# A hybrid decoder layer on one core: a scalar-engine root at the start, evacuations and column sums one by one behind low parts, and another pace in the first feed-forward stage

## The chip, the core and the metric

The kernel runs on one core of one Trainium2 chip. The metric is the device time in microseconds (us). A core has TensorE (PE in the profile, PEld for its weight loads), VectorE (DVE), ScalarE (ACT), GpSimd (POOL) and SyncE (SP, which here only starts DMAs). The engines run their own instruction streams in order and wait for one another by semaphores. PSUM is the memory in which TensorE accumulates; it has eight banks of 128 x 512 floats here.

## The reference, cut to what matters

```python
def swiglu(h, wg, wu, wd):
    return (jax.nn.silu(h @ wg) * (h @ wu)) @ wd

cond = jax.nn.silu(c)
mod = cond @ ada_w[l] + ada_b[l]                 # 9 vectors of 2048
sh1, sc1, gt1, sh2, sc2, gt2, sh3, sc3, gt3 = jnp.split(mod, N_MOD, axis=-1)
h = ada_in(x, norm_g[l, 0], sh1, sc1)            # rmsnorm(x) * (1 + sc1) + sh1
x = x + MACARON_W * gt1[:, None, :] * swiglu(h, ffn_w_gate[l, 0], ffn_w_up[l, 0], ffn_w_down[l, 0])
h = ada_in(x, norm_g[l, 1], sh2, sc2)
x = x + gt2[:, None, :] * hybrid_mixer(h, ...)   # two kinds of attention heads
h = ada_in(x, norm_g[l, 2], sh3, sc3)
x = x + MACARON_W * gt3[:, None, :] * swiglu(h, ffn_w_gate[l, 1], ...)
```

There are 256 tokens, a width of 2048 (16 slices of 128) and a feed-forward width of 5632 (44 slices), all in float32.

## The kernel before, in words

**Weights.** The weights come as 674 blocks of 512 KB, eight tiles of 128 x 128 each, in the order in which TensorE uses them (`Stream.next`, L136). SP starts the DMA of a block into `wraw` (L129), ACT rounds it to the high part `whi` (L133), DVE subtracts to get the low part `wlo` (L147). A product is then high by high, high by low and low by high. Each of the three tiles has four buffers, so the three steps can run some four blocks ahead of TensorE; `wraw` has a fifth. Blocks 0 and 1 are used whole, without parts (L630).

**Columns.** The vectors `mod` are made beside this: one column slice `adat` of 1 MB is fetched (L275) and DVE multiplies it by `cs` and sums it (L279, two rows in the profile, the second reads the sum out). There are 144 of them, 16 for each of nine vectors. `RATE` (L37) says how many columns are begun with each block from a given block on; `ada_need` begins those that are still missing. The columns of scale and shift of slice k make the k-th slice of `h` (`first_h`, L605: ACT, ACT, ACT, then the low part `hs` on DVE); `xrt` (L602) is `x` by its root, two slices at a time.

**Stages.** Blocks 0 to 111 are the gate and up products of the first 28 slices of the first feed-forward net (`gate_up_first`), blocks 112 to 167 its down product, 168 to 231 gate and up of the other 16 slices, 232 to 263 their down product. The mixer follows, then the second feed-forward net. In the first stage the slices of `h` come one by one with the columns, so the products of four groups of slices (8, 8, 8 and 4) are cut into `PIECES` (L24), each a group and the range of k that it adds. At the end of a piece its PSUM banks are emptied: ACT copies them to `acc` (L647) where k starts at 0, DVE adds them (L649, L651) otherwise. After the last piece of a slice come SiLU, the product of gate and up (L548) and the split into `hid` (L534 ACT, L535 DVE). Evacuations that are owed wait in the list `owed`, and `done` (L669) takes from it until at most n are left.

**Order.** The program is written in one order, and a scheduler with a model of its own sorts each engine's instructions by it; `issue_after` binds one instruction behind another. A changed wait can so move instructions far behind the edit.

**Start.** `fv` is the mean square of `x` for the first norm; its inverse root `fy` is made on DVE by `rsqrt` (L304 to L311, eight small instructions), while ACT makes `cs` (L744) and moves the transposed `x` (L769). `fy` becomes a row (`frb`, `nrow`). DVE sums the first two columns in halves (`first_col`, L780) and forms the first slice `h0` (L588, L589), on which TensorE's first product waits.

## Time and profile before

| what | value |
|---|---|
| median of 3 runs | 1918.75 us (1918.09 to 1921.13) |
| the profiled execution, its own time | 1916.67 us |
| its span from the first to the last instruction | 1914.9 us |
| PE busy | 1888.3 us (99%) |
| DVE busy | 1535.9 us (80%) |
| ACT busy | 1030.6 us (54%) |
| mean granted TensorE clock | 0.998 |

Busy TensorE is no TensorE at its peak: a matmul's end is modelled, and the next one starts before it. So the prediction counts the matmuls that begin in a stretch: in stretches of the same kind of product, fewer of them is time lost.

### The profile page before, as it was taken

Reading aid. Unit: us, or ns where it says so; the run is one execution under the profiler, and the core shown is the slowest. Engines: PE = TensorE matmul, PEld = TensorE weight load, DVE = VectorE, ACT = ScalarE, POOL = GpSimd, SP = SyncE. Lnnn points to the kernel's source line nnn. Section 1 sums busy time; section 2 is a strip of 40 time slices with the busy share of each in tenths; the row PEclk is TensorE's granted clock in tenths of the full one; section 3 lists DMA queues with packets and bytes.
Section 4 is the critical chain, followed back from the end, with each engine's and each line's share of the span. In section 5 each row is a group of like instructions: output and inputs, shape, how many; then the busy total and the mean of one; then the engine's idle time right before and its main releaser. Section 6 shows DMA issues by size and latency. Waiting matters only on the chain.

```text
span 1914.9 us, 33495 instructions
## 1 busy us (share of the span) xinstructions
PE 1888.3 (99%) x13090; PEld 1768.2 (92%) x13090; DVE 1535.9 (80%) x2243; ACT 1030.6 (54%) x1623; POOL 56.5 (3%) x50
## 2 busy tenths in 40 slices
PE   8999999999999999999999999999999999999998
PEld 7999999899999989989989999999999999999998
DVE  7999888998999997879978869977777656666654
ACT  8544545433554446756647656655554445555553
POOL 0000000000000120000000002000000000000011
PEclk9999999999999999999999999999999999999999
DMA  9999877999998986687677557777777666666653
GB/s 380 353 358 352 302 268 281 354 403 363 350 341 345 350 324 213 228 302 254 238 258 266 208 186 273 244 259 267 266 259 262 219 200 203 201 200 201 203 201 122
DMA packets 128913, 519.64 MB, mean 271 GB/s; under 512 B 18153, under 2 KB 21481, under 8 KB 110577
## 3 DMA queue, kind: packets, MB, share of 16 engines
q1 hardware_dynamic: 128754, 517.49, 75.2%
q8 instruction: 103, 1.69, 0.4%
q14 instruction: 56, 0.46, 0.1%
HBM read 512.96 MB, written 4.47 MB: 270 GB/s over the span
## 4 chain that ended last, share of the span: by engine, by line
PE 79%; DVE 11%; issue 3%; DMA 3%; ACT 3%; SPq 0%; DVEq 0%; ACTq 0%
PE pd L514 13%; PE pg L510 10%; PE pu L510 10%; PE pd L515 7%; PE pu L511 5%; PE pg L511 5%; DVE wlo L147 4%; PE pgu L635 3%; PE pgu L633 3%; PE pgu L634 3%; DVE adat L279 2%; PE pp L867 2%; PE pp L865 2%; PE pp L866 2%; PE po L514 2%
## 5 line engine op out<-in xcount | busy, mean ns | idle before, releaser
L147 DVE TENSOR_TENSOR wlo<-wraw,whi 128x1024 fp32r<-128x1024 f32 x672 | 819.6, 1226 | 271.8 <-ACT whi L133 270.7
L133 ACT CAST whi<-wraw 128x1024 fp32r<-128x1024 f32 x672 | 698.8, 1046 | 495.7 <-PE pd L514 181.8
L514 PE MATMUL pd<-hid,whi 128*128 128x512 f32 x1370 | 449.6, 382 | 0.8 <-DVE hid L535 0.8
L515 PE MATMUL pd<-hid,wlo 128*128 128x256 f32 x1370 | 374.4, 273 | 2.5 <-DVE wlo L147 2.5
L279 DVE CUSTOM_DVE_ANT_0 adat<-adat,cs,colt 128x2048 f32<-128x2048 f32 x142 | 335.5, 2363 | 11.9 <-DMA adat<-in_ada_dram 11.6
L510 PE MATMUL pg<-hs,whi 128*128 128x512 f32 x912 | 302.0, 382 | 0.5 <-DVE shc L459 0.5
L510 PE MATMUL pu<-hs,whi 128*128 128x512 f32 x912 | 301.8, 382 | 0.0
L514 PEld LDWEIGHTS pd<-hid,whi 128*128 128x128 f32 x1370 | 258.9, 189 | 36.9 <-DVE hid L535 1.1
L515 PEld LDWEIGHTS pd<-hid,wlo 128*128 128x128 f32 x1370 | 263.0, 192 | 5.1 <-DVE wlo L147 4.8
L511 PE MATMUL pu<-hs,wlo 128*128 128x256 f32 x912 | 248.6, 273 | 0.0
L511 PE MATMUL pg<-hs,wlo 128*128 128x256 f32 x912 | 248.6, 273 | 0.0
L633 PE MATMUL pgu<-hs,whi 128*128 128x256 f32 x880 | 241.6, 276 | 2.3 <-ACT whi L133 2.1
L634 PE MATMUL pgu<-hs,whi 128*128 128x256 f32 x880 | 240.9, 275 | 0.0
L635 PE MATMUL pgu<-hs,wlo 128*128 128x256 f32 x880 | 238.6, 276 | 2.2 <-DVE wlo L147 2.2
L510 PEld LDWEIGHTS pg<-hs,whi 128*128 128x128 f32 x912 | 172.4, 189 | 24.9 <-ACT shc L458 0.7
L510 PEld LDWEIGHTS pu<-hs,whi 128*128 128x128 f32 x912 | 172.4, 189 | 24.0
L865 PE MATMUL pp<-hs,whi 128*128 128x256 f32 x656 | 188.2, 288 | 0.0
L867 PE MATMUL pp<-hs,wlo 128*128 128x256 f32 x656 | 181.0, 276 | 1.4 <-DVE wlo L147 1.4
L866 PE MATMUL pp<-hs,whi 128*128 128x256 f32 x656 | 180.9, 276 | 0.0
L511 PEld LDWEIGHTS pu<-hs,wlo 128*128 128x128 f32 x912 | 175.1, 192 | 0.0
L511 PEld LDWEIGHTS pg<-hs,wlo 128*128 128x128 f32 x912 | 175.1, 192 | 0.0
L633 PEld LDWEIGHTS pgu<-hs,whi 128*128 128x128 f32 x880 | 168.9, 192 | 3.0 <-ACT whi L133 2.5
(338 smaller groups left out, 2587.0 us busy)
## 6 DMA issues: line engine op xcount, KB each, us to landing
wraw<-in_w_dram SPq DMA_DIRECT2D x674, 512.0 KB, 4.5
adat<-in_ada_dram SPq DMA_DIRECT2D x142, 1024.0 KB, 7.6
xr<-in_xr_dram SPq DMA_DIRECT2D x4, 512.0 KB, 5.1
adaf<-in_ada_dram SPq DMA_DIRECT2D x4, 512.0 KB, 8.2
xd<-x SPq DMA_DIRECT2D x4, 512.0 KB, 7.6
rw<-rowd SPq DMA_DIRECT2D x16, 128.0 KB, 6.5
x<-xd SPq DMA_DIRECT2D x4, 512.0 KB, 4.9
out_dram<-o SPq DMA_DIRECT2D x4, 512.0 KB, 3.6
```

Source lines behind the costliest of these rows:

```text
L133: self.cast = self.act = self.nc.scalar.copy(h, r).ins
L147: lo_ = nc.vector.tensor_tensor(self.l, r, self.h.bitcast(F32), ALU.subtract)
L279: W.sum = V.tensor_tensor_reduce(t, t, cs, 1.0, L("adab", q, 1), ALU.mult, ALU.add, mod[:, q : q + 1]).ins
L510: PE.matmul(ps, wt[0], both, start=(k == 0), stop=False)
L511: PE.matmul(ps[:, T:], wt[1], part(k, HI), start=False, stop=(k == KD - 1))
L514: PE.matmul(ps, wt[0], act.rearrange("p q (a b) -> p q b a", a=2), start=first, stop=False)
L515: PE.matmul(ps[:, :T], wt[1], woven(act[:, 0]), start=False, stop=last)
L633: PE.matmul(o, wh, part(k, HI), start=first and s == 0, stop=False, skip_group_check=skip)
L634: PE.matmul(o, wh, part(k, LO), start=False, stop=False, skip_group_check=skip)
L635: PE.matmul(o, wl, part(k, HI), start=False, stop=last, skip_group_check=skip)
L865: PE.matmul(pp[i][:, :T], wh, hh, start=(k == 0), stop=False)
L867: PE.matmul(pp[i][:, :T], wl, hh, start=False, stop=(k == KD - 1))
```

## The change

- `PIECES`: the fourth group takes k = 0 and 1 first and k = 2 with its next piece (before: k = 0 to 2, then from 3).
- `RATE`: other numbers up to block 264; the count of columns begun by then is 98 in both.
- Start: `fy` is a square root on ACT with one Newton step on DVE; the first half column stands ahead of that step, and the scaling of `gains_` is bound behind the first split.
- `W.late` is now set with the 33rd column (`i >= 2 * KD`), not with the mixer: from there a sum goes into the list `owing` and is written after a later block's low part. `BEHIND` is 1 until the mixer and 2 from there on (before: 2, in the mixer and behind it alone, since nothing was owed ahead of it). `ada_need` still empties the list wherever it is called.
- `done` takes at most one evacuation at a time where a piece runs slice by slice, and a last evacuation is bound behind the latest low part (`W.split`).

```diff
-    (0, 0, 1, 1), (1, 0, 1, 1), (2, 0, 2, 2), (3, 0, 3, 3), (0, 1, 4, 4), (1, 1, 6, 6), (3, 3, 7, 7),
+    (0, 0, 1, 1), (1, 0, 1, 1), (2, 0, 2, 2), (3, 0, 2, 2), (0, 1, 4, 4), (1, 1, 6, 6), (3, 2, 7, 7),
...
-RATE = ((0, 0.5), (8, 0.4), (50, 0.42), (75, 0.16), (112, 0.42), (168, 0.38), (232, 0.42), (264, 0.0), (284, 0.285), (376, 0.0), (424, 0.16))
+RATE = ((0, 0.44), (24, 0.41), (75, 0.2), (118, 0.42), (232, 0.3), (264, 0.0), (284, 0.285), (376, 0.0), (424, 0.16))
...
-BEHIND = 2
+BEHIND = (1, 2)
...
-                    self.settle(b - BEHIND)
+                    self.settle(b - BEHIND[self.quick])
...
         q = m * KD + j
+        W.late = i >= 2 * KD
...
+        with tc.issue_after(split0):
+            V.tensor_scalar(gains_, gains_, XS, None, ALU.mult)
...
-                V.tensor_add(acc[f], ps, acc[f])
+                with tc.issue_after(W.split):
+                    V.tensor_add(acc[f], ps, acc[f])
                 hids.append(swi(acc[f][:, :T], acc[f][:, T:], hp))
...
-            def done(f, n):
+            def done(f, n, most=NF):
                 owed.append(lambda ps=pb[f], k0=k0, k1=k1: evacuate(ps, f, k0, k1))
-                while len(owed) > n:
+                while len(owed) > n and most:
                     owed.pop(0)()
+                    most -= 1
...
-                    done(f, 1)
+                    done(f, 1, 1)
...
-    V.tensor_scalar(fv, fv, XS * XS / D, XS * XS * EPS, ALU.mult, ALU.add)
-    fy = rsqrt(fv, [P, 2], "x")
+    fy, fh, fa = (ep.tile([P, 2], F32, name=n) for n in ("fy", "fh", "fa"))
+    V.tensor_scalar(fh, fv, -0.5 * XS * XS / D, -0.5 * XS * XS * EPS, ALU.mult, ALU.add)
+    with tc.issue_after(hold):
+        hold = sqrt_table(L("eps")).ins
+    with tc.issue_after(hold):
+        hold = A.activation(fy, fv, AF.Sqrt, bias=L("eps"), scale=XS * XS / D).ins
...
-    first = rs["last"]
+    with tc.issue_after(first):
+        first = first_col(0, 0)
+    with tc.issue_after(first):
+        V.reciprocal(fy, fy)
+    V.tensor_tensor(fa, fy, fy, ALU.mult)
+    V.tensor_tensor(fa, fa, fh, ALU.mult)
+    first = V.scalar_tensor_tensor(fy, fa, 1.5, fy, ALU.add, ALU.mult).ins
...
-    for i, q in ((0, 0), (0, 1), (1, 0), (1, 1)):
+    for i, q in ((0, 1), (1, 0), (1, 1)):
         with tc.issue_after(first):
             first = first_col(i, q)
-    with tc.issue_after(first):
-        V.tensor_scalar(gains_, gains_, XS, None, ALU.mult)
...
-        W.late = True
+        W.quick = 1
```

Three places show what this does to the engines' own orders. First ACT, where TensorE is at blocks 8 to 11 (`acc<-pgu` is an evacuation of a bank, `whi` the rounding of a block, `g1f`, `ht` and `hs` make a slice of `h`). Before:

```order
L609 ACTIVATE g1f<-mod,colt 128x1
L133 CAST whi<-wraw 128x1024 x2
L610 ACTIVATE ht<-xrt,mod,g1f 128x256
L611 CAST hs<-ht 128x2x128
L647 COPY acc<-pgu 128x512 x8
L133 CAST whi<-wraw 128x1024 x3
```

and after:

```order
L612 CAST hs<-ht 128x2x128
L133 CAST whi<-wraw 128x1024
L648 COPY acc<-pgu 128x512 x5
L133 CAST whi<-wraw 128x1024
L648 COPY acc<-pgu 128x512 x3
L133 CAST whi<-wraw 128x1024
```

The eight evacuations of the third group stood in a row behind a slice of `h` and ahead of the casts of blocks 9 to 11; now the casts of blocks 8 and 9 stand between and behind them, and the slice of `h` (k = 2) comes later.

Second DVE from the low part of block 111 on, at the end of the first stage (`acc<-pgu,acc` evacuates, `acc<-acc` is gate by up, `hid` a low part of the result, the two ISA rows one column sum). Before:

```order
L147 TENSOR_TENSOR wlo<-wraw,whi 128x1024
L548 TENSOR_TENSOR acc<-acc 128x256
L279 ISA adat,mod<-adat,cs,colt 128x2048
L279 ISA mod 128x1
L535 TENSOR_TENSOR hid<-acc,hid 128x256
L651 TENSOR_TENSOR acc<-pgu,acc 128x512
L147 TENSOR_TENSOR wlo<-wraw,whi 128x1024
L548 TENSOR_TENSOR acc<-acc 128x256
L147 TENSOR_TENSOR wlo<-wraw,whi 128x1024
L535 TENSOR_TENSOR hid<-acc,hid 128x256
L651 TENSOR_TENSOR acc<-pgu,acc 128x512
L147 TENSOR_TENSOR wlo<-wraw,whi 128x1024
```

and after:

```order
L147 TENSOR_TENSOR wlo<-wraw,whi 128x1024
L547 TENSOR_TENSOR acc<-acc 128x256
L147 TENSOR_TENSOR wlo<-wraw,whi 128x1024
L534 TENSOR_TENSOR hid<-acc,hid 128x256
L653 TENSOR_TENSOR acc<-pgu,acc 128x512
L147 TENSOR_TENSOR wlo<-wraw,whi 128x1024
L547 TENSOR_TENSOR acc<-acc 128x256
L653 TENSOR_TENSOR acc<-pgu,acc 128x512
L534 TENSOR_TENSOR hid<-acc,hid 128x256
L280 ISA adat,mod<-adat,cs,colt 128x2048
L280 ISA mod 128x1
L547 TENSOR_TENSOR acc<-acc 128x256
```

The column sum stood ahead of the low part of block 112 and now stands behind that of block 113. From block 105 to 116 there were four sums (behind blocks 107, 111, 114 and 116), and now there is one (behind 113); another now stands ahead of block 105.

Third DVE from the low part of block 246 on, in the second down product (`x<-pd,mod,x` adds a result to `x`). Before:

```order
L147 TENSOR_TENSOR wlo<-wraw,whi 128x1024
L279 ISA adat,mod<-adat,cs,colt 128x2048
L279 ISA mod 128x1
L540 SCALAR_TENSOR_TENSOR x<-pd,mod,x 128x256
L147 TENSOR_TENSOR wlo<-wraw,whi 128x1024
L542 SCALAR_TENSOR_TENSOR x<-pd,mod,x 128x256
L147 TENSOR_TENSOR wlo<-wraw,whi 128x1024
L279 ISA adat,mod<-adat,cs,colt 128x2048
L279 ISA mod 128x1
L540 SCALAR_TENSOR_TENSOR x<-pd,mod,x 128x256
L147 TENSOR_TENSOR wlo<-wraw,whi 128x1024
L542 SCALAR_TENSOR_TENSOR x<-pd,mod,x 128x256
```

and after:

```order
L147 TENSOR_TENSOR wlo<-wraw,whi 128x1024
L541 SCALAR_TENSOR_TENSOR x<-pd,mod,x 128x256
L280 ISA adat,mod<-adat,cs,colt 128x2048
L280 ISA mod 128x1
L147 TENSOR_TENSOR wlo<-wraw,whi 128x1024 x2
L539 SCALAR_TENSOR_TENSOR x<-pd,mod,x 128x256
L280 ISA adat,mod<-adat,cs,colt 128x2048
L280 ISA mod 128x1
L541 SCALAR_TENSOR_TENSOR x<-pd,mod,x 128x256
L147 TENSOR_TENSOR wlo<-wraw,whi 128x1024 x2
L539 SCALAR_TENSOR_TENSOR x<-pd,mod,x 128x256
L147 TENSOR_TENSOR wlo<-wraw,whi 128x1024
```

Here the sums move behind the low parts by a little. Over the whole stage, from block 232 to 263, there are eleven sums before and nine after.

## Rows read from the trace of the kernel before

**Rows 1.** The page, first part: busy us, share of the span, instructions.
```profile
PE 1888.3 (99%) x13090; PEld 1768.2 (92%) x13090; DVE 1535.9 (80%) x2243; ACT 1030.6 (54%) x1623; POOL 56.5 (3%) x50
```

**Rows 2.** Stretches: their length, busy us of PE, PEld, DVE, ACT, POOL (instructions), clock, DMA.
```profile
26.00:106.00 80.00, 76.70 (x674) 75.66 (x673) 74.49 (x79) 47.10 (x69) 0.00 (x0) 1.00 0.90 354
120.00:200.00 80.00, 80.00 (x719) 80.00 (x718) 74.35 (x77) 38.35 (x49) 0.00 (x0) 1.00 0.96 376
236.00:316.00 80.00, 79.25 (x709) 79.02 (x708) 67.14 (x86) 39.40 (x59) 0.00 (x0) 1.00 0.75 262
350.00:410.00 60.00, 60.00 (x368) 55.24 (x367) 54.47 (x55) 24.16 (x23) 0.00 (x0) 1.00 0.98 383
660.00:720.00 60.00, 57.87 (x346) 51.72 (x345) 58.31 (x63) 27.05 (x36) 15.99 (x11) 1.00 0.90 332
```

**Rows 3.** PE's waits from 26 to 106 us: total us, times, longest.
```profile
PE pgu L633 <- ACT whi L133: 2.1, 2, 1.4
PE pgu L635 <- DVE wlo L147: 1.1, 1, 1.1
```

**Rows 4.** PE's waits from 236 to 316 us.
```profile
PE pgu L635 <- DVE wlo L147: 0.8, 1, 0.8
```

**Rows 5.** PE's waits from 300 to 340 us.
```profile
PE pd L514 <- DVE hid L535: 0.8, 1, 0.8
PE pgu L635 <- DVE wlo L147: 0.4, 1, 0.4
PE pd L515 <- DVE wlo L147: 0.4, 2, 0.2
```

**Rows 6.** Timeline of the start: start us, us, engine, line, operation.
```profile
9.05 2.04 ACT L744 ACTIVATE cs<-pcs 128x512 f32<-128x512 f32 x4
...
12.45 1.29 DVE L780 CUSTOM_DVE_ANT_0 adaf<-adaf,cs,colt 128x1024 f32<-128x1024 f32 x1
...
18.42 0.16 DVE L815 TENSOR_SCALAR colt<-colt 128x2 f32<-128x2 f32 x1
18.54 0.35 DVE L589 TENSOR_SCALAR h<-h,mod 128x256 f32<-128x256 f32 x1
...
19.00 7.14 PE L630 MATMUL pgu<-h,wraw 128*128 128x256 f32 x32 [1.07 <-issue]
```

**Rows 7.** The tile of the first columns: its DMAs' issue, and their time to landing.
```profile
L234 SPq DMA_DIRECT2D adaf<-in_ada_dram x4: 445/463/715, 3.7 to 5.4; - x4
...
DMA to landing us min/median/max: 7.7/8.2/9.9
```

**Rows 8.** ACT's timeline around a table load in the second down product.
```profile
696.46 0.42 ACT L328 ACTIVATE sq<-x 128x256 f32<-128x256 f32 x1 [3.51 <-DVE x L542]
696.89 1.28 ACT L319 ACT_TABLE_LOAD   x1
698.19 0.20 ACT L319 ACTIVATE dummy<-x 128x1 f32<-128x1 f32 x1
```

**Rows 9.** ACT's timeline from 41.8 to 47 us.
```profile
41.43 4.00 ACT L647 COPY acc<-pgu 128x512 f32<-128x512 f32 x8
45.25 2.06 ACT L133 CAST whi<-wraw 128x1024 fp32r<-128x1024 f32 x2
```

**Rows 10.** DVE's groups, 19 to 113 us: busy us, mean ns, idle before and releaser.
```profile
L147 DVE TENSOR_TENSOR wlo<-wraw,whi 128x1024 fp32r<-128x1024 f32 x32 | 38.3, 1225 | 6.0 <-ACT whi L133 6.0
L279 DVE CUSTOM_DVE_ANT_0 adat<-adat,cs,colt 128x2048 f32<-128x2048 f32 x14 | 32.9, 2349 | 0.0
L649 DVE TENSOR_TENSOR acc<-pgu,acc 128x512 f32<-128x512 f32 x20 | 12.7, 688 | 0.4 <-PE pgu L635 0.3
```

**Rows 11.** DVE's groups from 660 to 715 us.
```profile
L147 DVE TENSOR_TENSOR wlo<-wraw,whi 128x1024 fp32r<-128x1024 f32 x20 | 26.4, 1326 | 0.3 <-ACT whi L133 0.3
L279 DVE CUSTOM_DVE_ANT_0 adat<-adat,cs,colt 128x2048 f32<-128x2048 f32 x9 | 23.5, 2608 | 0.0
```

**Rows 12.** PE's longest wait in the mixer, from 738 to 1140 us.
```profile
PE ppt L1225 <- ACT x L1220: 2.2, 2, 2.0
```

More of the change, by code (lines that the diff above doesn't have):

```diff
@@ L109, in __init__ @@
         self.first = []
-        self.late, self.owing = False, []
+        self.late, self.owing, self.quick = False, [], 0
     def settle(self, upto=N_TILES):
@@ L294, in layer_kernel @@
     W.side = ada_col
-    rs = {}
     def rsqrt(v, shape, name):
@@ L310, in rsqrt @@
         V.scalar_tensor_tensor(a, a, -10.0 / 3.0, a, ALU.add, ALU.mult)
-        rs["last"] = V.scalar_tensor_tensor(y, a, 5.0, y, ALU.add, ALU.mult).ins
+        V.scalar_tensor_tensor(y, a, 5.0, y, ALU.add, ALU.mult)
         return y
@@ L758, in layer_kernel @@
     V.tensor_tensor(fv[:, :1], ss[:, 0, :1], ss[:, 0, 1:], ALU.add)
-    V.tensor_tensor_reduce(junk2, last_half, last_half, 1.0, ss[:, 1, :1], ALU.mult, ALU.add, fv[:, 1:])
-    V.tensor_scalar(fv, fv, XS * XS / D, XS * XS * EPS, ALU.mult, ALU.add)
-    fy = rsqrt(fv, [P, 2], "x")
+    first = V.tensor_tensor_reduce(junk2, last_half, last_half, 1.0, ss[:, 1, :1], ALU.mult, ALU.add, fv[:, 1:]).ins
+    fy, fh, fa = (ep.tile([P, 2], F32, name=n) for n in ("fy", "fh", "fa"))
[4 more added lines that the diff above has]
+        hold = A.activation(fy, fv, AF.Sqrt, bias=L("eps"), scale=XS * XS / D).ins
     def features(i):
```

## Prediction

> **What bounds the kernel now.** I read the page's first lines first [rows 1]: TensorE (PE) is busy for 99% of the span, VectorE (DVE) for 80%, ScalarE (ACT) for 54%. So PE is the bound, and the change takes no matmul away. It can win only the time before PE's first product and the gaps between products. How much that is, busy time does not tell, because a matmul's end is modelled. I therefore counted the matmuls that start in stretches of equal length and equal kind [rows 2]. In the first stage 80 us hold 719 where nothing is late (120 to 200), which is 80 / 719 = 0.111 us for one. From 26 to 106 they hold 674: 45 fewer, 45 x 0.111 = 5.0 us lost. From 236 to 316 they hold 709: 10 fewer, 1.1 us lost. In the down products 60 us hold 368 undisturbed (350 to 410), 0.163 us each, and only 346 from 660 to 720: 22 x 0.163 = 3.6 us lost.
>
> Then I read what PE waits for in these places. From 26 to 106 it is ACT's `whi` (2.1 us in two waits) and DVE's `wlo` (1.1 us) [rows 3]. From 236 to 316 it is one wait of 0.8 us for `wlo` [rows 4], against 1.1 us by the count, so a wait costs about 0.3 us more than its row shows. From 300 to 340, where the first stage turns into its down product, there are four waits of 1.6 us in all, for DVE's `hid` and `wlo` [rows 5], which by the same surcharge is 1.6 + 4 x 0.3 = 2.8 us. In the second down product DVE is busy for 58.31 of 60 us [rows 2]: there DVE is the engine with no room. So nearly all that can be won lies in DVE's order and load, some at the start, and one piece on ACT.
>
> **The change part by part.**
>
> Start. PE's first product begins at 19.00, right behind the first slice `h` (18.54 + 0.35), which stands behind the two half sums of the first column and the scaling of `gains_` [rows 6]. The half sums start at 12.45, when DVE has ended the eight-step root. The first half could begin at its landing: issued at 3.7, 7.7 us at the fastest [rows 7], so at 11.4. Now one half sum goes first, and the root comes from ACT. ACT ends `cs` at 9.05 + 2.04 = 11.09, must then load a table, 1.28 us by the load seen later [rows 8], so 12.37, and a dummy (0.20) and the root (taken like the dummy) end at about 12.8. The half sum ends at 11.4 + 1.29 = 12.7. Four small steps of about 0.16 to 0.2 us follow on DVE, and the second half sum starts at about 13.5. It would have started at 12.45 + 1.29 = 13.74 before. That is 0.2 us sooner, the scaling of `gains_` (18.42 to 18.54, 0.12) leaves the path, and I take **0.4 us** gained. Ends: 1.0 us gained, if the half sum's 1.05 us (12.45 - 11.4) come through whole; 1.0 us lost, if the half column lands at the slowest 9.9 us (13.6), and the root waits behind it.
>
> On the table load a rule speaks against this. Rows first: the load starts 0.01 us after ACT's instruction before it, and the dummy 0.02 us after the load [rows 8], so the load is all that a switch costs here. The Trainium skill, "ScalarE: Activation LUTs", section "What ACT_TABLE_LOAD costs", puts a drain of the pipeline of about 1.38 us beside the load. The trace does not agree with it at this place; by that figure the root would be 1.4 us later.
>
> Blocks 2 to 33 (about 19 to 113 us). DVE's work is the same in both orders: 32 low parts of 1.23 us, 14 column sums of 2.35, 20 evacuations of 0.69 [rows 10], in another sequence. The one clear gap is on ACT: eight evacuations take from 41.43 to 45.43, ahead of the casts of `whi` for blocks 9 to 11 [rows 9], and PE waits up to 1.4 us there [rows 3]; with the surcharge the two `whi` waits are 2.1 + 0.6 = 2.7 us. In the changed order the casts stand between the evacuations, and that gap should go. But DVE's groups add to 38.3 + 32.9 + 12.7 = 83.9 us [rows 10], and a block is 24 matmuls, 24 x 0.111 = 2.67 us of PE, so 32 blocks are 85.4 us. DVE's idle here is only 6.0 us, all of it waiting for `whi` [rows 10]. A gap taken out at 46 us is thus mostly met again later, when the same DVE work has not been done in time. I keep **1.0 us** of the 2.7. Ends: nothing, and 2.5 us.
>
> Blocks 75 to 83 (236 to 247 us). A burst of evacuations, products, splits and a column sum on DVE delays one `wlo` [rows 4]. Evacuations now come one at a time behind low parts, with a sum a block later: **0.9** of 1.1 us gained. Ends 0 and 1.1.
>
> Blocks 104 to 116. Four column sums become one, so three sums of some 2.35 us leave DVE just where PE waits for `hid` and `wlo`. `hid` itself still waits for PE's last gate and up product and for SiLU, so not all goes: I take **1.9** of 2.8 us. Ends 0 and 2.8. The sums go to blocks 75 to 104 and to the first down product, which lies beside undisturbed work; from 120 to 200 us DVE has 80 - 74.35 = 5.65 us free while PE waits for nothing [rows 2].
>
> Second down product (blocks 232 to 263). Eleven sums become nine. In 55 us of it DVE runs 20 low parts of 1.33 us and 9 sums of 2.61 us [rows 11], longer than in the first stage; 2 x 2.61 = 5.2 us leave DVE, while PE loses 3.6 us there because DVE is full. That covers the loss, if the lead is not spent where a sum and an evacuation meet; I take **2.8** of 3.6 us. Ends 1.0 and 3.6. The two sums are made up before it, at blocks 168 to 231, where 23 other column starts become 24 to 26, and PE shows no wait.
>
> Behind it. Every weight block, column count and stage is the same from block 264 on, but the scheduler sets the mixer's instructions in another order, with one more pair of table loads (2 x 1.28 us on ACT). PE's longest wait there is 2.0 us for an ACT step [rows 12]. One such wait may go or come: **0**, with 2.0 us and a half to either side.
>
> Sum: 0.4 + 1.0 + 0.9 + 1.9 + 2.8 + 0 = 7.0 us. The profiled execution took 1916.67 us, so 1909.7 by its own time; it was 2.1 us under the median of the runs, 1918.75. I set the gain against the median: **1911.8 us**.
>
> **The rivals.**
>
> Less than that, and no measurable change. DVE keeps 74.5 of 80 us in the first stage [rows 2] whatever the order. If the sums that left blocks 105 to 116 and the second down product only push the same DVE shortage ahead of them, or the mixer's new order gives back a wait of 2.5 us, only the start, blocks 2 to 33 and blocks 75 to 83 remain: 0.4 + 1.0 + 0.9 = 2.3 us, 1916.4. With both the first-stage gains and a lost 2.5 us it is 1918.9. For it: PE's gaps are small and spread, and in a full stretch a gap removed comes back. Against it: in both places where most is forecast, work does leave DVE, it is not only put elsewhere in the same stretch.
>
> That the change does not do what it says: `ada_need` still empties the list of owed sums, at every slice of `h` in the first stage, so some sums stand there as before, ahead of the low part. Where that happens blocks 2 to 33 and 75 to 83 bring nothing: 7.0 - 1.9 = 5.1 us, 1913.6, still faster.
>
> Slower: lumps on DVE. In the new order of blocks 2 to 33, five evacuations and a column sum stand in a row ahead of the low parts of blocks 16 and 26, four and a sum ahead of that of block 32: 5 x 0.69 + 2.35 + 1.23 = 7.0 us from one low part's end to the next, against 2.67 us of PE's pace for a block. If DVE has no lead there, PE waits 7.0 - 2.67 = 4.4 us at each of the two, and 0.7 less at the third: 12.5 us where PE loses 5.0 us now, 7.5 us more. With blocks 75 to 83 and the transition no better either, and only the 2.8 us of the second down product gained, the time would be 1918.75 + 7.5 - 2.8 = 1923.4. It decides at a lead of about 4.4 us of the low parts of blocks 15 and 25 over PE. Against it: the buffers allow a lead of four blocks, 10 us, and at PE's waits for `wlo` from 26 to 106 there is one of 1.1 us only [rows 3], so the lead is usually there.
>
> The drain at the table switch, beside the load: ACT's root is then later by as much as the load's own length again, 1.28 us, and so is the first product: 7.0 - 1.3 = 5.7, **1913.0**. Against it speaks that the row shows no pause around the load [rows 8]. The page of the Trainium skill named above would have it so, by its figure with 1.38 us for 1.28.
>
> **How the numbers follow.** The forecast has .53, the one that some sums do not move (1913.6) .06, the drain (1913.0) .05, no measurable change .27, the lumps .09. What a measurement of this kernel can tell from no change is about 0.2%, 3.8 us: faster means under 1914.9, slower over 1922.6. Faster .53 + .06 + .05 = .64, same .27, slower .09. Range: the upper ends of the terms are 1.0 + 2.5 + 1.1 + 2.8 + 3.6 = 11.0 us, which would not all come together; about 10 of them gives 1908.8. At the top it goes to 1917.5, past the 2.3 us case (1916.4), leaving out the lumps and the worse half of "no change".
>
> **What would show it.** Right: PE's first product at 18.5 to 18.7; the evacuations of the third group in two runs and no `whi` wait near 46 us; over 700 matmuls from 26 to 106 only if DVE's shortage is not met again, some 683 by my term; no wait over 0.5 us from 300 to 340; over 360 matmuls from 660 to 720, with DVE under 56 of 60 us. Wrong: waits for `wlo` of 2 us and more at blocks 16, 26 or 32 (the lumps), new waits in the mixer as long as the gain, DVE still over 58 us from 660 to 720, or a first product later than 19.0.

## The result: slower by 0.5%, and where the time went

The changed kernel takes 1930.69 us (median of 6 runs, 1928.32 to 1931.64), the kernel before 1919.3 us in the same comparison. The ratio is 1.0053, with a 95% interval of 1.004 to 1.0067. The forecast was 1911.8 us, faster; the time lies outside its range. The profiled execution of the changed kernel took 1931.64 us with a span of 1929.8, 14.9 us more than the 1914.9 of before. By the medians the change costs 11.4 us. The six executions of the changed kernel spread over 3.3 us and the six of the kernel before over 6.7, and a profile is one of them, so the stretches below say where time goes and the medians how much it is.

The page of the changed kernel, first part (busy us, share of the span, instructions), answers [rows 1]:

```profile
PE 1896.3 (98%) x13090; PEld 1772.8 (92%) x13090; DVE 1532.1 (79%) x2239; ACT 1036.6 (54%) x1629; POOL 54.5 (3%) x50
```

The stretches of the changed kernel answer [rows 2] (length, busy us of PE, PEld, DVE, ACT and POOL with instructions, clock, DMA share, GB/s):

```profile
26.00:106.00 80.00, 78.19 (x675) 76.09 (x674) 73.41 (x78) 47.53 (x69) 0.00 (x0) 1.00 0.92 359
120.00:200.00 80.00, 78.75 (x701) 78.25 (x701) 74.74 (x76) 37.59 (x48) 0.00 (x0) 1.00 0.92 361
236.00:316.00 80.00, 75.01 (x664) 74.44 (x663) 67.54 (x91) 39.51 (x62) 0.00 (x0) 1.00 0.72 253
350.00:410.00 60.00, 60.00 (x368) 55.14 (x367) 53.59 (x54) 24.14 (x23) 0.00 (x0) 1.00 0.98 374
660.00:720.00 60.00, 60.00 (x368) 55.15 (x368) 56.78 (x61) 30.02 (x38) 10.93 (x9) 1.00 0.89 340
```

From 660 to 720 us there are 368 matmuls for 346, as forecast, though the two rows do not hold the same part of the second down product: it begins at 644 us before and at 660 in the changed kernel. The table below compares like with like. From 26 to 106 there are 675 for 674, so nothing was won. From 120 to 200, where nothing had been forecast, 719 fell to 701, and 236 to 316 fell from 709 to 664, where a gain had been forecast.

Both kernels run 13090 matmuls of the same kinds in the same stages. So I compared when the n-th of them begins. The table gives, for one stretch after another, how much longer (+) or shorter the changed kernel and the experiments took than before, in us, from one profile each (in four profiles one matmul's record is missing, which moves an entry by up to 0.1). The stretches are named by their times in the kernel before: start and first blocks to 26, blocks 2 to 33 to 116, then to 245; the end of the first stage and the turn into its down product, 278 to 340; first down product and six blocks behind it to 493; 54 of blocks 168 to 231, 493 to 635; the last three of them and the second down product, 635 to 734; the mixer to 1128 and its output projection to 1220. From 245 to 278 no kernel differs. Behind 1220 only `after_old_late` (+0.87), `head_pace_020` (+0.54) and `second_down_032_mixer_031` (+3.84) differ by over 0.1.

| kernel | to 26 | to 116 | to 245 | 278-340 | to 493 | to 635 | to 734 | to 1128 | to 1220 |
|---|---|---|---|---|---|---|---|---|---|
| changed | -0.06 | +0.47 | +0.95 | +4.66 | 0 | +9.74 | -3.50 | +2.74 | 0 |
| after_old_late | -0.62 | +0.53 | +0.95 | +5.06 | 0 | +2.46 | -3.32 | +1.56 | 0 |
| after_old_rate | +0.61 | -1.90 | +0.03 | +1.37 | 0 | 0 | +0.26 | -0.54 | 0 |
| after_old_evac | -0.21 | +0.53 | +7.42 | +3.93 | 0 | +9.74 | -3.33 | -0.69 | 0 |
| before_new_late | +0.26 | +0.04 | 0 | +1.98 | +0.91 | 0 | +0.28 | +1.53 | 0 |
| second_down_036 | -0.54 | -1.98 | +0.02 | +3.24 | +0.35 | 0 | -1.77 | +0.13 | +3.95 |
| second_down_038 | +0.82 | -1.98 | +0.03 | +1.66 | 0 | 0 | -0.16 | +3.08 | +3.42 |
| new_head_old_tail_pace | -0.69 | +0.44 | +0.95 | +2.76 | 0 | 0 | -0.15 | +0.96 | +0.33 |
| old_head_new_tail_pace | +0.68 | -1.97 | +0.02 | +0.44 | 0 | +10.83 | -1.83 | +4.41 | +3.33 |
| head_pace_020 | -0.55 | -1.98 | +0.02 | +1.05 | 0 | 0 | +0.36 | +4.33 | -0.23 |
| old_rate_old_pieces | -0.50 | +1.31 | -1.02 | +0.37 | 0 | 0 | +0.15 | -0.30 | 0 |
| more_in_first_down | -0.08 | -1.99 | +0.03 | +0.93 | +3.00 | +2.98 | -3.56 | +1.29 | 0 |
| new_tail_two_behind | +0.64 | -1.98 | +0.03 | +2.52 | +1.13 | +3.92 | -2.14 | +4.26 | +3.42 |
| new_tail_pace_040 | -0.76 | -1.98 | +0.03 | +0.26 | 0 | +5.91 | -1.56 | +1.23 | +4.24 |
| less_in_second_down | -0.81 | -1.96 | +0.03 | +0.55 | 0 | 0 | -3.54 | +5.75 | +0.33 |
| second_down_030 | -0.36 | -1.99 | +0.02 | -0.14 | 0 | 0 | -3.57 | +2.10 | +7.14 |
| second_down_034 | +0.20 | -1.98 | +0.03 | +0.71 | 0 | 0 | -3.03 | +1.79 | +3.04 |
| second_down_034_mixer_031 | -0.01 | -1.99 | +0.02 | +2.90 | +0.68 | 0 | -3.03 | +6.72 | 0 |
| second_down_032_mixer_031 | -0.65 | -1.99 | +0.03 | -0.55 | 0 | 0 | -3.51 | +2.35 | 0 |

The first row adds to +15.0. Two stretches come to nearly as much: +9.74 in blocks 168 to 231, where PE had waited for nothing, and +4.66 around the end of the first stage.

How much of an entry is the execution and not the kernel can be read from kernels in which DVE and ACT run the same instructions in the same order through a stretch. In `after_old_rate` and nine others (`new_tail_pace_040`, `old_head_new_tail_pace` and all of experiment 5 but `more_in_first_down`) the orders are the same from block 2 to 167, and yet 278 to 340 runs from -0.55 to +3.24. PE's granted clock tells them apart: from 333 to 345 us it is 0.86 in the four with the most (`after_old_rate`, `second_down_036`, `second_down_038` and `second_down_034_mixer_031`, +1.37 to +3.24) and 1.00 in the six others (-0.55 to +0.71), though PE waits 1.9 to 2.4 us for `hid` there in all ten. The stretch in `after_old_rate` and `second_down_034`:

```profile
333.00:345.00 12.00, 9.81 (x50) 8.53 (x49) 10.77 (x13) 3.53 (x4) 0.00 (x0) 0.86 0.91 330
```
```profile
333.00:345.00 12.00, 9.66 (x60) 8.63 (x59) 11.78 (x14) 4.51 (x6) 0.00 (x0) 1.00 0.89 335
```

In the mixer the changed kernel, `after_old_late` and `after_old_evac` have one order and take +2.74, +1.56 and -0.69; from 905 to 920 us the clock is 0.89 in the first two and 1.00 in the third. The start is one and the same in all rows but `before_new_late` and runs from -0.81 to +0.82. So an entry of these three columns can be off by some 1 us at the start and 2 to 4 us in the others. From 493 to 635 kernels with one order agree: +9.74 twice, and 0 in all ten with the order of `after_old_rate`.

**Blocks 168 to 231.** PE's waits from 493 to 660 us in the changed kernel (total us, times, longest):

```profile
PE pg L510 <- DVE wlo L147: 3.4, 5, 0.9
PE pu L510 <- DVE wlo L147: 2.3, 4, 0.9
```

PE waits for low parts, and yet DVE is not full. From 535 to 640 us the kernel before, the changed one and `after_old_late` (the change without its late sums, experiment 1) show:

```profile
535.00:640.00 105.00, 105.00 (x643) 96.54 (x642) 95.16 (x111) 52.97 (x80) 0.00 (x0) 1.00 0.92 354
```
```profile
535.00:640.00 105.00, 100.15 (x593) 89.02 (x593) 91.72 (x107) 49.47 (x75) 0.00 (x0) 1.00 0.90 340
```
```profile
535.00:640.00 105.00, 104.88 (x633) 95.10 (x632) 98.13 (x115) 53.56 (x80) 0.00 (x0) 1.00 0.96 363
```

DVE is *less* busy in the changed kernel (91.72 us for 95.16) while PE waits for it. The two engines of the low parts wait for each other instead. For a gate or up product ACT copies one half out of PSUM (`mg`), DVE adds the other half (`tg` or `tu`, L527), ACT takes SiLU of `tg` (L546), DVE multiplies the two (L547), and ACT splits the result (`hid`). DVE's timeline of the changed kernel (start, us, line, operation, idle before), a little left out at either side:

```profile
593.59 0.42 DVE L527 TENSOR_TENSOR tu<-pu,mg 128x256 f32<-128x256 f32 x1 [0.42 <-ACT mg L526]
593.93 2.34 DVE L280 CUSTOM_DVE_ANT_0 adat<-adat,cs,colt 128x2048 f32<-128x2048 f32 x1
...
596.20 0.42 DVE L547 TENSOR_TENSOR tu<-tu,tg 128x256 f32<-128x256 f32 x1
```

and ACT's in the same stretch:

```profile
593.18 0.37 ACT L526 COPY mg<-pu 128x256 f32<-128x256 f32 x1 [1.27 <-PE pu L510]
593.45 1.05 ACT L133 CAST whi<-wraw 128x1024 fp32r<-128x1024 f32 x1
596.65 0.43 ACT L533 CAST hid<-tu 128x256 fp32r<-128x256 f32 x1 [2.15 <-DVE tu L547]
```

The column sum stands between the addition and the product that make `tu`, and ACT waits 2.15 us for the product. What such a wait does to the casts of weights behind it in ACT's queue shows 15 us later, where a sum (608.76 to 611.03) and a low part stand ahead of the addition `tg`; rows of DVE, then of ACT, then PE's:

```profile
612.17 0.42 DVE L527 TENSOR_TENSOR tg<-pg,mg 128x256 f32<-128x256 f32 x1
614.01 1.23 DVE L147 TENSOR_TENSOR wlo<-wraw,whi 128x1024 fp32r<-128x1024 f32 x1 [1.42 <-ACT whi L133]
615.15 2.35 DVE L280 CUSTOM_DVE_ANT_0 adat<-adat,cs,colt 128x2048 f32<-128x2048 f32 x1
617.76 1.22 DVE L147 TENSOR_TENSOR wlo<-wraw,whi 128x1024 fp32r<-128x1024 f32 x1
...
612.62 0.42 ACT L546 ACTIVATE tg<-tg 128x256 f32<-128x256 f32 x1 [2.62 <-DVE tg L527]
612.95 1.98 ACT L133 CAST whi<-wraw 128x1024 fp32r<-128x1024 f32 x2
...
619.03 0.38 PE L510 MATMUL pg<-hs,wlo 128*128 128x256 f32 x1 [0.85 <-DVE wlo L147]
```

ACT waits 2.62 us for `tg`, and the casts stand behind that wait. DVE waits 1.42 us for the first of these casts, runs the next sum, and PE waits 0.85 us for the low part behind it. Over 493 to 660 us ACT's waits for DVE in the changed kernel, and DVE's for ACT's casts, are

```profile
ACT hid L533 <- DVE tu L547: 22.5, 12, 3.0
ACT tg L546 <- DVE tg L527: 16.3, 9, 3.1
DVE wlo L147 <- ACT whi L133: 9.3, 13, 1.4
```

against 13.2 and 3.9 us of ACT's, with a longest of 1.6, and 4.5 us of DVE's, with a longest of 0.5, in the kernel before:

```profile
ACT hid L534 <- DVE tu L548: 13.2, 13, 1.6
DVE wlo L147 <- ACT whi L133: 4.5, 12, 0.5
```

**The end of the first stage.** Here a sum stands ahead of a product too, and its own column has not landed. DVE and then ACT of the changed kernel:

```profile
291.16 0.68 DVE L653 TENSOR_TENSOR acc<-pgu,acc 128x512 f32<-128x512 f32 x1
295.09 2.35 DVE L280 CUSTOM_DVE_ANT_0 adat<-adat,cs,colt 128x2048 f32<-128x2048 f32 x1 [3.24 <-DMA adat<-in_ada_dram]
...
297.37 0.42 DVE L547 TENSOR_TENSOR acc<-acc 128x256 f32<-128x256 f32 x1
297.70 1.22 DVE L147 TENSOR_TENSOR wlo<-wraw,whi 128x1024 fp32r<-128x1024 f32 x1
```
```profile
297.82 0.42 ACT L533 CAST hid<-acc 128x256 fp32r<-128x256 f32 x1 [5.52 <-DVE acc L547]
298.15 1.04 ACT L133 CAST whi<-wraw 128x1024 fp32r<-128x1024 f32 x1
```

DVE idles 3.24 us for the column and sums it in 2.35. ACT, which needs the product behind the sum, idles 5.52 us with the next cast queued behind. From 234 to 330 us DVE waits four times for a column, 9.9 us in all; in the kernel before twice, 3.8 us. From 276 to 325 us PE waits three times, 5.0 us in all:

```profile
PE pgu L636 <- DVE wlo L147: 5.0, 3, 2.5
```

After the longest of these waits PE's granted clock falls from 2.4 GHz to a mean of 0.66 of that over five us, so part of these at 1.2 GHz, and only 28 matmuls begin there where 47 or 48 do in five us at full clock beside it:

```profile
310.00:315.00 5.00, 2.64 (x24) 2.45 (x22) 4.30 (x5) 0.69 (x2) 0.00 (x0) 1.00 0.27 108
315.00:320.00 5.00, 4.82 (x28) 4.82 (x29) 4.43 (x8) 2.75 (x5) 0.00 (x0) 0.66 0.63 209
320.00:325.00 5.00, 5.00 (x47) 5.00 (x47) 4.23 (x6) 3.00 (x5) 0.00 (x0) 1.00 0.88 331
```

In `new_head_old_tail_pace`, which has the same order here, the same three waits take 4.7 us, the clock stays at 1.00, and the stretch takes +2.76 for +4.66. So 1.9 us of the changed kernel's loss go with the clock.

### The profile page after: what moved, and what is told of

Same layout as the page of the kernel before. It is cut to its first block, busy times and chain, and to the rows that moved or that the text cites. A ratio compares the mean times of both kernels' runs of the same rounds, so it can differ in the third digit from the quotient of the medians.

```text
span 1929.8 us, 33528 instructions
## 1 busy us (share of the span) xinstructions
PE 1896.3 (98%) x13090; PEld 1772.8 (92%) x13090; DVE 1532.1 (79%) x2239; ACT 1036.6 (54%) x1629; POOL 54.5 (3%) x50
## 4 chain that ended last, share of the span: by engine, by line
PE 77%; DVE 11%; issue 4%; DMA 4%; ACT 3%; SPq 1%; DVEq 0%; ACTq 0%
PE pd L513 16%; PE pu L509 9%; PE pg L509 9%; PE pd L514 8%; PE pu L510 5%; PE pg L510 5%; DVE wlo L147 4%; PE pgu L636 3%; PE pgu L635 3%; PE pgu L634 3%; DVE adat L280 3%; PE po L513 2%; PE pp L876 2%; PE pp L877 2%; PE pp L878 2%
## 5 line engine op out<-in xcount | busy, mean ns | idle before, releaser
L634 PE MATMUL pgu<-hs,whi 128*128 128x256 f32 x880 | 240.6, 277 | 0.6 <-ACT whi L133 0.3
L509 PEld LDWEIGHTS pg<-hs,whi 128*128 128x128 f32 x912 | 172.4, 189 | 24.5 <-ACT shc L457 0.7
L636 PEld LDWEIGHTS pgu<-hs,wlo 128*128 128x128 f32 x880 | 166.3, 193 | 10.2 <-DVE wlo L147 10.1
```

What stands on the lines that cost most here:

```text
L509: PE.matmul(ps, wt[0], both, start=(k == 0), stop=False)
L634: PE.matmul(o, wh, part(k, HI), start=first and s == 0, stop=False, skip_group_check=skip)
L636: PE.matmul(o, wl, part(k, HI), start=False, stop=last, skip_group_check=skip)
```

## The experiments

Each is the changed kernel with the edit shown, or the kernel before with one part. Ratios are to the kernel before.

**1. One part undone, or one alone.** The late sums undone (`after_old_late`):

```diff
-BEHIND = (1, 2)
+BEHIND = 2
...
-                    self.settle(b - BEHIND[self.quick])
+                    self.settle(b - BEHIND)
...
-        W.late = i >= 2 * KD
...
-        W.quick = 1
+        W.late = True
```

> The changed kernel with one part undone: column sums are written where they are begun up to the mixer, as before (W.late only in the mixer, BEHIND 2). Theory A (the late sum): a sum a block later stands on VectorE ahead of the gate-by-up product that ScalarE waits for, and ScalarE's next casts of weights stand behind that wait. Then the waits for wlo at 280 to 320 us and in blocks 168 to 231 (about 6.4 and 9.7 us more than before) go: 1913 to 1918 us. Theory B (the pace: more columns begun in blocks 168 to 231): blocks 168 to 231 still lose 6 us or more, 1925 us or more. Theory C (the bound and one-by-one evacuations): little moves, 1928 to 1932.

Measured: 1922.32 us, 1.0018 (1.0007 to 1.003), between the ranges of A and B and in neither. Blocks 168 to 231 lose 2.46 us in place of 9.74, and the end of the first stage keeps its loss.

The pace undone (`after_old_rate`):

```diff
-RATE = ((0, 0.44), (24, 0.41), (75, 0.2), (118, 0.42), (232, 0.3), (264, 0.0), (284, 0.285), ...)
+RATE = ((0, 0.5), (8, 0.4), (50, 0.42), (75, 0.16), (112, 0.42), (168, 0.38), (232, 0.42), (264, 0.0), (284, 0.285), ...)
```

> The changed kernel with the RATE of before. Theory A (the late sum): blocks 168 to 231 keep at least 6 of their 9.7 us, and the 3.5 us that the second down product gained are lost again as it has eleven sums: 1928 to 1936 us. Theory B (the pace): blocks 168 to 231 lose under 2 us, the second down product loses its gain: 1921 to 1926 us. Theory C (the evacuations): as A here.

Measured: 1916.68 us, 0.9986 (0.9975 to 0.9997), better than any of the theories had it and faster than the kernel before. Blocks 168 to 231 lose nothing although the sums are late. Theory A by itself falls.

The evacuations undone (`after_old_evac`):

```diff
-                with tc.issue_after(W.split):
-                    V.tensor_add(acc[f], ps, acc[f])
+                V.tensor_add(acc[f], ps, acc[f])
...
-                    done(f, 1, 1)
+                    done(f, 1)
```

> The changed kernel with the evacuations of before (no limit of one at a time, the last evacuation not bound behind a low part). Theory C (the evacuations stand in the wrong place): the 6.4 us lost at 280 to 320 us shrink by at least 4, 1923 to 1927 us. Theories A and B: within 2 us of the changed kernel, 1928.5 to 1932.5, and the waits at 280 to 320 stay.

Measured: 1935.4 us, 1.008 (1.006 to 1.0099): slower still, and over the range of A and B too; theory C falls. Without the limit DVE runs five evacuations, six products and a column sum between two low parts from 232 to 240.6 us, and PE waits 4.6 us there (205 to 250 us):

```profile
PE pgu L636 <- DVE wlo L147: 4.6, 1, 4.6
```

In that stretch the two edits to the evacuations gain 6.5 us (+0.95 for +7.42); which of the two does it was not tried.

The late sums alone, in the kernel before (`before_new_late`; the lines of `after_old_late`, the other way round, with `quick` 0 at the start):

> The kernel before with one part of the change alone: sums owed from the 33rd column on and written a block later (BEHIND 1 up to the mixer). Theory A (the late sum): blocks 168 to 231, where PE waits for nothing before, lose 6 us or more, the end of the first stage 3 or more: 1927 to 1935 us. Theories B and C: within 2 us of 1919.

Measured: 1920.31 us, 1.0002 (0.9993 to 1.0012). At the pace of before, late sums cost nothing in blocks 168 to 231. So late sums and the new pace cost most together: 0 us there for the late sums alone, 2.46 for the pace without late sums, 9.74 for both.

**2. Which part of the pace.** `new_head_old_tail_pace` and `old_head_new_tail_pace` (the pace ahead of block 112 or 168, and behind):

```diff
-(118, 0.42), (232, 0.3), (264, 0.0),
+(118, 0.42), (168, 0.38), (232, 0.42), (264, 0.0),
```
```diff
-RATE = ((0, 0.44), (24, 0.41), (75, 0.2), (118, 0.42), (232, 0.3),
+RATE = ((0, 0.5), (8, 0.4), (50, 0.42), (75, 0.16), (112, 0.42), (232, 0.3),
```

> The changed kernel with the pace of before from block 168 on (0.38, then 0.42), the new pace ahead of it. Theory P (two separate places): the new pace of the first stage costs its 6 us up to block 168, blocks 168 to 231 lose nothing at 0.38, the second down product gains nothing at 0.42: 1923 to 1928 us. Theory Q (the loss in blocks 168 to 231 is inherited: sums arrive in a bad phase from the first stage): blocks 168 to 231 still lose 6 us or more: 1931 to 1938 us.

Measured: 1922.05 us, 1.0012 (1.0003 to 1.0022), 1 us under P's range: nothing lost in blocks 168 to 231, and blocks 2 to 33 without the gain of `after_old_rate`. The first stage costs less than P's 6 us: the order of DVE and ACT is that of the changed kernel up to block 167, but 278 to 340 takes +2.76 here.

> The changed kernel with the pace of before up to block 167 and the new one behind it (0.42 from 112 to 231, 0.30 from 232). Theory P: nothing lost from 280 to 325 us, blocks 168 to 231 lose some 10 us at 0.42, the second down product gains some 4: 1921 to 1926 us. Theory Q: blocks 168 to 231 lose under 3 us: 1912 to 1916 us.

Measured: 1935.21 us, 1.0082 (1.0062 to 1.0103): blocks 168 to 231 lose 10.83 us, though the first stage loses nothing. Theory P holds in both places, Q falls. The total is larger than P had it, by 4.41 us in the mixer and 3.33 in the output projection.

`head_pace_020` keeps the pace of before but for one number, `(75, 0.2)` for `(75, 0.16)`:

> The changed kernel with the pace of before everywhere but from block 75 on, where the new 0.20 stands for 0.16. If the pace of 0.20 itself (seven sums for six in blocks 75 to 111) causes the loss of some 5 us from 278 to 325 us seen with the new first-stage pace: that loss appears here, 1920 to 1923 us. If it comes from which blocks the sums fall on (the other numbers of the first stage shift them): it stays away, 1915 to 1918 us.

Measured: 1922.47 us, 1.0011 (1.0 to 1.0022), in the range of the first theory, but not by its loss. Nothing up to 300 us; then one wait of 1.9 us (DVE waits 5.3 us for columns from 276 to 340). From 278 to 318, ahead of the turn, this kernel takes +3.0 us with a clock of 0.91 from 305 to 325, the changed one +6.6 with the same clock, and `new_head_old_tail_pace` +4.7 with 1.00; the ten profiles of the old pace with one order run from -0.8 to +1.2. So 0.20 makes one of the waits, and the others of the first stage's new numbers, which move the sums to other blocks, must make the rest. In the turn, where fewer sums fall, about 2 us come back, and the net +1.05 is within what the old pace itself shows (-0.55 to +3.24). The kernel's larger part, +4.33, lies in the mixer (below).

**3. The place of the sum, or DVE's load.** Both change `old_head_new_tail_pace`: `new_tail_two_behind` sets `BEHIND = (2, 2)`, and `new_tail_pace_040` adds `(168, 0.40)` to the pace, with sums one block later.

> The kernel with the old first-stage pace and the new one from block 112 on, with owed sums two blocks behind (BEHIND 2 throughout) in place of one. If the place of the sum among ScalarE's partners causes the 10 us of blocks 168 to 231: they change by more than 3 us either way. If the load on VectorE causes them: they stay within 2 us of 10, about 1933 to 1937 us.

Measured: 1928.38 us, 1.0037 (1.0022 to 1.0052).

> As the kernel with the old first-stage pace and the new one behind it, but 0.40 for 0.42 in blocks 168 to 231 (0.42 lost 10 us there, 0.38 nothing). If VectorE's load decides it and grows evenly: about half, 4 to 6 us lost there. If there is an edge below which nothing waits: under 2 us, or all 10.

Measured: 1924.9 us, 1.0026 (1.0016 to 1.0036). The table sets the loss in blocks 168 to 231 beside the column sums that DVE runs in that stretch (493 to 635 us of the kernel before), ACT's waits for DVE's results (`hid` and `tg` together, 493 to 660 us) and DVE's waits for ACT's casts (`wlo` for `whi`, in all and longest, 493 to 660 us):

| kernel | pace | sum | sums | ACT's waits, us | DVE's waits, us | loss, us |
|---|---|---|---|---|---|---|
| before | 0.38 | at once | 20 | 17.1 | 4.5, 0.5 | 0 |
| before_new_late | 0.38 | one block later | 20 | 22.0 | 3.2, 0.6 | 0 |
| new_head_old_tail_pace | 0.38 | one block later | 21 | 35.6 | 6.1, 0.5 | 0 |
| after_old_late | 0.42 | at once | 23 | 21.1 | 5.2, 0.5 | 2.46 |
| new_tail_two_behind | 0.42 | two blocks later | 22 | 24.5 | 5.4, 0.6 | 3.92 |
| new_tail_pace_040 | 0.40 | one block later | 21 | 42.2 | 9.8, 1.4 | 5.91 |
| changed | 0.42 | one block later | 22 | 38.8 | 9.3, 1.4 | 9.74 |
| old_head_new_tail_pace | 0.42 | one block later | 23 | 52.2 | 11.9, 1.4 | 10.83 |

Rows on which two lines rest, first of `old_head_new_tail_pace`, then of `new_tail_two_behind`:

```profile
ACT hid L533 <- DVE tu L547: 33.8, 14, 3.0
ACT tg L546 <- DVE tg L527: 18.4, 10, 3.1
DVE wlo L147 <- ACT whi L133: 11.9, 18, 1.4
```
```profile
ACT hid L533 <- DVE tu L547: 18.1, 14, 2.2
ACT tg L546 <- DVE tg L527: 6.4, 5, 1.5
DVE wlo L147 <- ACT whi L133: 5.4, 14, 0.6
```

The same columns begun with the same blocks, but summed one block further behind, halve both engines' waits and take 7 of the 10.8 us away; summed at once in place of one block later, they take 7.3 of the changed kernel's 9.74. So the place decides most. Between 0.38 and 0.42 with sums one block later the loss grows evenly (0, 5.91, 10.83), as the expectation had it for DVE's load, but the load alone does not give it: 21 sums one block later lose nothing in `new_head_old_tail_pace` and 5.91 us in `new_tail_pace_040`, where they fall on other blocks, and 23 at once lose 2.46 where 23 one block later lose 10.83. The waits of ACT alone are no sure measure, as 35.6 us cost nothing. The losses over 5 us go with casts that come late for DVE (9 to 12 us, longest 1.4; elsewhere 3 to 6 us, longest 0.6).

**4. The pieces.** `old_rate_old_pieces` is `after_old_rate` with

```diff
-    ... (3, 0, 2, 2), (0, 1, 4, 4), (1, 1, 6, 6), (3, 2, 7, 7),
+    ... (3, 0, 3, 3), (0, 1, 4, 4), (1, 1, 6, 6), (3, 3, 7, 7),
```

> The changed kernel with the pace and the PIECES of before. If the cut of the pieces makes the gain of about 2 us in blocks 2 to 33: that stretch loses it again, 1918 to 1921 us. If the evacuations one at a time make it: 1915.5 to 1918 us, as with the new pieces.

Measured: 1919.06 us, 1.0003 (0.9993 to 1.0014). Blocks 2 to 33 take 3.2 us more than with the new pieces (+1.31 against -1.90), so the cut makes that gain; the stretch to 245 us gives 1.05 back. Not all of the 3.2 is the pieces' own: PE's clock here is 0.72 from 46 to 52 us, behind its two waits for `whi`. The kernel before and `before_new_late`, with the same order, waits of 2.1 us for `whi` and a clock of 1.00, take 0 and +0.04, which leaves 1.9.

**5. Keeping the gain of the second down product.** All have the pace of before up to block 231 unless said:

```diff
 less_in_second_down        (232, 0.30), (284, 0.32)
 more_in_first_down         (112, 0.46), (168, 0.38), (232, 0.34), (284, 0.285)
 second_down_036            (232, 0.36), (284, 0.285)
 second_down_038            (232, 0.38), (284, 0.285)
 second_down_030            (232, 0.30), (284, 0.285)
 second_down_034            (232, 0.34), (284, 0.30)
 second_down_034_mixer_031  (232, 0.34), (284, 0.31)
 second_down_032_mixer_031  (232, 0.32), (284, 0.31)
```

> The changed kernel with the pace of before, but 0.30 in place of 0.42 from block 232 on and 0.32 in place of 0.285 from block 284 on, where VectorE has room. Theory P: the gains of the first stage stay (1916.7 with the pace of before), the second down product gains some 3.5 us by its fewer sums and nothing is lost ahead of it: 1911 to 1915 us. If sums moved into the mixer cost as much there as they bring: 1916 to 1919 us.

Measured: 1921.34 us, 1.0007 (0.9997 to 1.0016), over both ranges. 3.54 us gained in the second down product, 5.75 lost in the mixer, with one wait ahead of 860 us that the kernel before does not have:

```profile
PE pp L876 <- ACT whi L133: 2.8, 1, 2.8
```

> The changed kernel with the pace of before up to block 111, 0.46 in the first down product, 0.38 in blocks 168 to 231 and 0.34 from 232 on (98 columns by block 264 again, two of the second down product's moved to the first). If the first down product has room for two more sums: nothing lost from 340 to 460 us, some 3.5 us gained from 660 to 720, 1912 to 1915 us. If it has none, 0.46 there acts as 0.42 does in blocks 168 to 231: 1919 us or more.

Measured: 1919.48 us, 0.9995 (0.9983 to 1.0007). The first down product has no room for 0.46: 3.00 us lost there, and 2.98 in blocks 168 to 231.

> As second_down_036 with 0.30: eight sums, 95 columns, and 0.285 from block 284 on as before (in less_in_second_down it was 0.32). If the 6 us that less_in_second_down lost in the mixer came from the higher pace there, they are gone: 1911 to 1914 us. If they came from the mixer's new order, a loss of 2 us or more can be seen somewhere in it though the pace is that of before: 1914 to 1920.

Measured: 1922.73 us, 1.0017 (1.0006 to 1.0028), over both ranges. The wait of 2.8 us is gone and the mixer loses 2.10 in place of 5.75. (In `less_in_second_down` the clock was 0.84 from 845 to 866 us, here 1.00.) But 7.14 us are lost in the output projection, where DVE now runs seven sums for four. PE's waits from 1125 to 1250 us:

```profile
PE po L514 <- DVE wlo L147: 2.7, 3, 1.2
PE pg L452 <- DVE wlo L147: 1.9, 1, 1.9
PE nsum L348 <- ACT sq L327: 1.7, 1, 1.7
```

The columns left out by block 264 must be there for the next norm, and `ada_need` begins them all at once.

> As second_down_036 with 0.34 and 0.30 from block 284 on: nine sums. The gain of the second down product 2 to 4 us; the mixer by its order alone, as there: 1912 to 1920 us.

Measured: 1917.7 us, 0.9983 (0.9973 to 0.9993), the lowest ratio of all, though 3.04 us are lost in the output projection.

> The changed kernel with the pace of before, but 0.36 for 0.42 from block 232 on: nine sums there for eleven, 96 columns by block 264 for 98, the pace behind it unchanged. The gain of the second down product should be 2 to 4 us. If the mixer's time follows the order in which the scheduler sets it and not the columns it holds, it may still move by up to 6 us either way: 1912 to 1920 us; without that, 1912 to 1915.

Measured: 1919.24 us, 0.9996 (0.9987 to 1.0005). 1.77 us are gained in the second down product, under the 2 expected, and 3.95 lost in the output projection; the mixer itself stays.

> As second_down_036 with 0.38: ten sums, 97 columns. The gain of the second down product 0.5 to 2.5 us; the mixer is set nearest to that of the kernel with the pace of before, so it should move by under 2 us: 1914 to 1917 us.

Measured: 1921.5 us, 1.001 (1.0 to 1.002): no gain in the second down product at ten columns begun there, 3.08 us lost in the mixer and 3.42 in the output projection, all against the expectation.

> As second_down_034 with 0.31 in place of 0.30 from block 284 on. If the 3 us lost at the end of the mixer's output projection (1130 to 1225 us) are columns that were not begun in time: one column more begun by then, and the loss is under 1 us. The second down product keeps its gain of some 3.5 us; the mixer's order is a new one, which has moved it by 0 to 6 us. 1912 to 1916 us if the order does little, 1916 to 1920 if not.

Measured: 1921.88 us, 1.0015 (1.0006 to 1.0024), over both ranges. The loss in the output projection is gone (0 for +3.04), as expected; the mixer now takes +6.72, the 2.8 us wait for `whi` among it and a clock of 0.89 from 845 to 866 us behind it.

> The same with 0.32 from block 232 on: the same expectations, in one more order of the mixer: 1912 to 1916 us if the order does little, 1916 to 1920 if not.

Measured: 1916.73 us, 0.9991 (0.9982 to 1.0). Here 4.3 us of gain last to the end of the output projection; 3.84 of it go at the first turn of the second feed-forward net, where again a sum waits for its column (2.3 us) ahead of a product that `hid` needs.

## Why the prediction was wrong, step by step

**Start.** The half sum started at 11.42, the root ended by 12.73 and the second half sum began at 13.44, all as worked out. (In the kernel before it began at 13.87, not at the 13.74 of the sum.) The table load shows no drain: its 1.28 us, and the dummy 0.02 us behind it.

```profile
11.05 1.28 ACT L318 ACT_TABLE_LOAD   x1
...
12.35 0.20 ACT L318 ACTIVATE dummy<-colt 128x1 f32<-128x1 f32 x1
12.45 0.28 ACT L768 ACTIVATE fy<-fv,colt 128x2 f32<-128x2 f32 x1
...
13.44 1.28 DVE L787 CUSTOM_DVE_ANT_0 adaf<-adaf,cs,part 128x1024 f32<-128x1024 f32 x1
...
16.36 0.37 ACT L817 COPY nrow<-nrow 128x256 f32<-128x256 f32 x1 [1.62 <-PE nrow L813]
...
16.76 0.48 DVE L587 SCALAR_TENSOR_TENSOR h<-x,g,nrow 128x256 f32<-128x256 f32 x1 [0.64 <-ACT nrow L817]
...
18.49 0.35 DVE L588 TENSOR_SCALAR h<-h,mod 128x256 f32<-128x256 f32 x1
```

The rival of the drain falls, and with it the figure of 1.38 us that the Trainium skill, "ScalarE: Activation LUTs", section "What ACT_TABLE_LOAD costs", sets beside the load: here it is not seen. In this profile the gain was 0.05 us, not 0.4 (18.49 for 18.54): the row `nrow`, which PE now makes behind all the products that transpose `x`, became late, and the slice `h` waits 0.64 us for it. But one profile misleads here. Over the 18 profiles with this start PE's first product begins at 18.19 to 19.82 us, with a median of 18.70, and at 19.00 and 19.23 in the two with the old one, so 0.4 us is borne out in the middle. In eight of the 18 `h` waits 0.3 us or more for `nrow`, at most 1.27; the prediction did not ask what would be late next there.

**Blocks 2 to 33.** Forecast -1.0, measured +0.47. The gap of the eight evacuations at 46 us went as said, and the new pieces are worth 1.9 to 3.2 us by experiment 4. The new pace takes 2.4 back (-1.90 with the old pace). The lump ahead of block 16 is there as read (five evacuations and a sum, 60.72 to 65.98 us), but PE waits 0.6 us for that low part, not 4.4, and waits for none at blocks 26 and 32. Another lump stands near 150 us (five evacuations, a sum, two more evacuations) and costs about 1.4 us.

**Blocks 75 to 83.** Forecast -0.9, measured -1.02. Right, and by the evacuations one by one: it is there in `old_rate_old_pieces` and not in `before_new_late`. (In the table it is within the stretch to 245, where the lump near 150 us and 0.5 us behind it offset it.)

**Blocks 104 to 116.** Forecast -1.9; the turn itself gained 1.97. The step that failed is the sentence behind it, that the sums go to blocks 75 to 104 and to DVE's free time. They were priced at nothing there. At 279 to 313 us three sums stand in DVE's queue before their columns have landed (2.79, 3.24 and 2.78 us of wait), ahead of steps on which ACT and its casts wait: +6.6 us ahead of the turn and +4.66 net in this profile, +4.7 and +2.76 in the other one with the same order and the clock at 1.00, where the six profiles of the old pace at 1.00 have -0.55 to +0.71 net.

**Second down product.** Forecast -2.8 of at most 3.6, measured -3.50. Right, and the starts did go from eleven to nine.

**Blocks 168 to 231.** This is the step that decided it: "the two sums are made up before it, at blocks 168 to 231, where 23 other column starts become 24 to 26, and PE shows no wait", priced at nothing. It cost 9.74 us. That PE waits for nothing there was read as room. DVE's 91% busy share there was near what this chain of ACT and DVE can bear: more sums alone cost 2.46, and the sum's new place between the steps of a hand-over took the rest. (The counts in that sentence were wrong too: column starts there went from 25 to 26, and the other of the two went to blocks 75 to 111, 7 for 6.)

**Mixer.** Forecast 0 with 2.0 to 2.5 us to either side, measured +2.74, just outside; but the same order of DVE and ACT took +1.56 and -0.69 in two other kernels, the last with the clock at 1.00 throughout, so the forecast is not refuted here. In the experiments it runs from -0.7 to +6.7.

**The rivals.** "Slower" had the right engine and kind (DVE's work in a row ahead of low parts) and the wrong place and price. The rival that DVE's shortage is only pushed ahead was the nearest, but it was held to take back gains, not to cost 14 us; its argument against itself, that work does leave DVE in both places, forgot that it arrives somewhere.

What stays open: which of the first stage's other numbers makes the two waits ahead of the turn that 0.20 alone does not (4.7 us in three waits for 1.9 in one); and how much of the mixer's time is its order and how much the clock. The eight kernels of experiment 5 moved it by 0.1 to 6.7 us with nearly the same work, but one and the same order spreads over 3.4 us, and each of the eight was profiled once.

Two versions are faster than both kernels by a little, each by less than the 0.2% that the prediction took as the least that can be told: the change with the pace of before, 0.9986 (0.9975 to 0.9997), and the same with 0.34 from block 232 and 0.30 from block 284, 0.9983 (0.9973 to 0.9993). Their intervals overlap, and they are the best of 18 that were run.

## What to carry to other kernels

Work that is moved must be priced where it arrives, even if the consumer shows no wait there: a stage without waits may have no slack, and here one more column begun in 64 blocks, with the sums in a worse place, cost four times a sum's length. Where two in-order engines hand tiles back and forth, look at what stands between two steps of one hand-over: an engine can be less busy than before and still be what the consumer waits for. A quantity that must be complete at some point cannot be saved by a slower pace; what is not made up on the way comes back in a lump at that point. And before a stretch of one profile is read as an effect, look how far two profiles with the same order differ there, and at their granted clock.
